# A transformer encoder on one core: the sums of the second and third down steps each wait for another pair's split

## The chip, the cores and the metric

The kernel runs on 1 core of one Trainium2 chip. The metric is the device time of one execution in microseconds (us); lower is better. A program on a core drives several engines that run side by side, each with an in-order queue of its own: TensorE (PE; its weight loads are listed as PEld), VectorE (DVE), ScalarE (ACT), GpSimd (POOL) and SyncE (SP), the last of which only issues DMA transfers here.

## The reference

Two encoder layers over 256 tokens of width 2048. Each layer has a token mixer (neighbourhood attention in the first, grouped-query attention in the second) beside cross-attention to 256 memory tokens, one output projection, and then a dense MLP with a squared ReLU. The change is in the MLP:

```python
        n = rms_norm(h, mlp_norm[i])
        h = h + jnp.square(jax.nn.relu(n @ w_up[i])) @ w_down[i]
```

`w_up` is 2048 x 8192 and `w_down` 8192 x 2048, in float32.

## The kernel before, in words

**Split products.** Every float32 operand is split into a rounded high part (ACT copies it to the reduced type) and the residual (DVE subtracts the high part from the original); the helper `split` does both, so all its rows carry lines L507 (ACT) and L508 (DVE). A product is then three matmuls: high x high, high x low, low x high. Names end accordingly: `uh`/`ul` for the up weights, `bh`/`bl` and `th`/`tl` for the down weights, `a_s` for the activations.

**The up products.** `w_up` comes in 64 chunks of 128 features (`up_grains`). A chunk is loaded to `raw_U`, split in two halves, and multiplied in 48 matmuls of 128x256 (L411) into `ps_u`. Then ACT applies ReLU and square (L1113, L1114) into a tile `c`. Two consecutive chunks make a **pair**; when its second chunk is done, `squared` forms sums and differences of its four 128x128 blocks on DVE (L1122 to L1124) and splits them into `a_s`. The residual of that split (on DVE) is the instruction that the program notes in `box["made"]`.

**The down products.** Most of `w_down` is done by a Strassen scheme: 60 down **steps** (`down_grains`, numbered n from 0), each with one pair and one 1024-column half of the output. A step loads a tile `b` of four 128x512 blocks and makes a tile `t` of four sums from it: one block by an ACT copy (L1165) and an accumulating DMA issued by POOL (L1166), the other three by DVE in a chain, L1172, L1173, L1174, each reading the one before. Three blocks of `b` are split into `bh`, `bl` and used in the step's first half (9 matmuls of 128x512 on PE); the four sums are split into `th`, `tl` and used in its second half (12 matmuls; L1195, L1198 and L1199 are the three matmuls of a product). The products go to seven accumulators `p1` to `p7` in PSUM. When the output half changes, they are evacuated by ACT (copies to `z`, L1250) and by DVE (L1241). The buffers of `bh`, `bl`, `th` and `tl` are single: the next step's split waits until PE has read the last one. `t` has two buffers, `b` three.

**The order of work.** The MLP begins with four up chunks; from then on step n is interleaved with one up chunk: first half of the step, two halves of up chunk n + 4, second half. PE's order is pinned (`keep_in_program_order`). On the other engines a scheduler of the framework orders the instructions when the kernel is built, from its own estimate of the times; `tc.issue_after(x)` forbids it to put the instructions inside it ahead of instruction x on the same engine. It is used in `pre`, where the first of the three sums (L1172) is built, for n = 1 and n = 2, the second and the third step: L1173 and L1174 follow it through their data. Step n takes the pair j of `STEPS[n]`; the run lengths in `RUNS` begin with two steps on one output half and then alternate by four, so the first steps use the pairs 0, 1, 0, 1, 2, 3.

Of the kernel before, what the change touches and what calls it, by code (L numbers as in the profile page):

```python
# [159 lines left out]
def encoder_kernel(ctx: ExitStack, tc: tile.TileContext, t: dict, out: bass.AP):  # L160
# [206 lines left out]
    def later(n, fn, *args):  # L367
        pending.append((state["tick"] + n, fn, args))
# [136 lines left out]
    def split(dst_hi, dst_lo, src):  # L505

        first = nc.scalar.activation(dst_hi, src, AF.Copy)  # L507
        return first, nc.vector.tensor_tensor(dst_lo, src, dst_hi.bitcast(F32), op=ALU.subtract)  # L508
# [422 lines left out]
    def past(fn, ins=None):  # L931

        a, v = ins or box["ready"]
        with tc.issue_after(a.ins), tc.issue_after(v.ins):
            fn()
# [112 lines left out]
    def up_grains(layer, m):  # L1048
# [50 lines left out]
        def after():  # L1099
            squared(layer, m, own["ps"])  # L1100
# [5 lines left out]
    def squared(layer, m, ps):  # L1106

        e = m % 2
        if e == 0:
            box["c"] = at.mlp.tile([P, 8, P], F32, tag="c", bufs=2, name="c")  # L1110
        c = box["c"]
        two = c[:, 2 * e : 2 * e + 2, :].rearrange("p a b -> p (a b)")
        box["relu"] = nc.scalar.activation(two, ps, AF.Relu)  # L1113
        nc.scalar.activation(two, two, AF.Square)  # L1114
        if e == 0:
            return
        pair = m // 2
        if pair >= max(STEPPED):
            a = at.mlp.tile([P, 2, 4, P], F32R, tag="a", bufs=6, name="a_p")
            split(a[:, 0], a[:, 1], c[:, :4])  # L1120
        else:
            nc.vector.tensor_tensor(c[:, 4, :], c[:, 0, :], c[:, 2, :], op=ALU.subtract)  # L1122
            nc.vector.tensor_tensor(c[:, 5:7, :], c[:, 0:8:4, :], c[:, None, 1, :].to_broadcast([P, 2, P]), op=ALU.add)
            nc.vector.tensor_tensor(c[:, 7, :], c[:, 3, :], c[:, 6, :], op=ALU.subtract)  # L1124
            a = at.mlp.tile([P, 2, 7, P], F32R, tag="a", bufs=6, name="a_s")
            box["made"] = split(a[:, 0], a[:, 1], c[:, 1:])[1]
            if pair >= min(STEPPED):

                n = pair - min(STEPPED)
                if n == 0:  # L1130
                    box["a_0"] = at.mlp.tile([P, max(STEPPED) - min(STEPPED), 2, P], F32R, tag="a", bufs=6, name="a_0")
                split(box["a_0"][:, n, 0], box["a_0"][:, n, 1], c[:, 0])
        box["a", pair] = a
        if m == UPS - 1 and layer == 1:
            later(2, load_gf)
# [11 lines left out]
    def down_grains(layer, n, begins, ends, sooner):  # L1147

        q, j = STEPS[n]
        own = {}  # L1150

        def load():
            own["b"] = at.side.tile([P, 4, 512], F32, tag="b", bufs=3, name="b")
            nc.sync.dma_start(own["b"].rearrange("p a b -> p (a b)"),
                              t[f"w_pair{layer}"][j * 2 + q])

        def behind(fn, far=4):

            return (lambda: past(fn, box["splits"][-far])) if n < 2 else fn

        def lift():

            b, s = own["b"], at.side.tile([P, 4, 512], F32, tag="T", bufs=2, name="t")
            own["t"] = s
            nc.scalar.activation(s[:, 3, :], b[:, 3, :], AF.Copy)  # L1165
            nc.gpsimd.dma_start(s[:, 3, :], b[:, 1, :], accum_op=ALU.add)  # L1166

        def pre():

            b, s = own["b"], own["t"]  # L1170
            with tc.issue_after(box["made"].ins) if n in (1, 2) else nullcontext():
                nc.vector.tensor_tensor(s[:, 0, :], b[:, 3, :], b[:, 0, :], op=ALU.add)  # L1172
            nc.vector.tensor_tensor(s[:, 1, :], s[:, 0, :], b[:, 1, :], op=ALU.add)  # L1173
            nc.vector.tensor_tensor(s[:, 2, :], s[:, 1, :], b[:, 2, :], op=ALU.add)  # L1174

        def prep_first():
            own["first"] = tuple(at.mlp.tile([P, 3 * 512], F32R, tag=x, name=x) for x in ("bh", "bl"))
            split(*own["first"], own["b"].rearrange("p a b -> p (a b)")[:, : 3 * 512])

        def prep_second():  # L1180
            own["second"] = tuple(at.mlp.tile([P, CH], F32R, tag=x, name=x) for x in ("th", "tl"))
            with tc.issue_after(box["relu"].ins) if n == 0 else nullcontext():
                split(*own["second"], own["t"].rearrange("p a b -> p (a b)"))

        def run(which, products):
            if n == 0 and which == "first":
                open_strassen(layer)
            hi, lo = own.pop(which)
            a = box["a", j]
            for name, ai, bi in products:  # L1190
                if n == 0:
                    sum_of(name)
                entered = begins and not (name in SHARED and q in box["z_set"])
                ps, s = box["ps"][name], slice(bi * 512, (bi + 1) * 512)
                ins = nc.tensor.matmul(ps, a[:, 0, ai, :], hi[:, s], start=entered, stop=False,  # L1195
                                       skip_group_check=True)
                pin(ins)
                nc.tensor.matmul(ps, a[:, 0, ai, :], lo[:, s], start=False, stop=False, skip_group_check=True)  # L1198
                nc.tensor.matmul(ps, a[:, 1, ai, :], hi[:, s], start=False, stop=ends, skip_group_check=True)  # L1199

        def after(products):
            if ends:
                for name, _, _ in products:
                    taken(q, name)
                    if n + 1 < len(STEPS):
                        seeded(STEPS[n + 1][0], name)

        def after_second():
            after(SECOND)
            if ends:  # L1210
                box["z_set"].add(q)
            if ends and j == STEPPED[q] - 1:
                folded(q, 0.5 if n == len(STEPS) - 1 else 1)

        return [Grain(lambda: run("first", FIRST), lambda: after(FIRST), load, behind(pre), behind(prep_first, 4 if n else 1),
                      (8 if n < 2 else 12, 8 if sooner else 5, 4), behind(lift)),
                Grain(lambda: run("second", SECOND), after_second, None, None, behind(prep_second), SOONER)]

    def open_strassen(layer):

        closed(*[x for x in reversed(list(pools)) if x in ("ps_acc", "ps_att")])
        at.sums = opened("ps_sums", space=bass.MemoryType.PSUM)
        first = ["p3", "p5", "p1", "p2"]
        second = ["up"] + [x[0] for x in SECOND[:3]]
        box["ps"], box["unused"] = {}, set()
        for x in first + second if layer else second + first:
            box["ps"][x] = at.sums.tile([P, 512], F32, tag=x, name="ps_u" if x == "up" else x)
            box["unused"].add(x)

    def sum_of(name):  # L1230
        if name in box["unused"]:
            box["unused"].remove(name)
        else:
            box["ps"][name] = at.sums.tile([P, 512], F32, tag=name, name="ps_u" if name == "up" else name)
        return box["ps"][name]
# [7 lines left out]
    def taken(q, name):  # L1243

        ps, inv = box["ps"][name], box["inv"]
        if name in DIRECT:
            i, b = DIRECT[name]
            add_scaled(columns_of(i, q, b), ps, inv[:, i : i + 1])
            return
        nc.scalar.activation(box["z"][q][:, SHARED.index(name), :], ps, AF.Copy)  # L1250

    def seeded(q, name):

        ps = sum_of(name)
        if name in SHARED and q in box["z_set"]:
            nc.scalar.activation(ps, box["z"][q][:, SHARED.index(name), :], AF.Copy)
# [524 lines left out]
```

## Time and profile before

| what | value |
|---|---|
| median of 3 runs | 2002.78 us (2001.56 to 2003.46) |
| the profiled execution, time | 2002.76 us |
| its span | 2001.0 us |
| mean granted clock of TensorE | 0.997 |
| PE busy | 1984.8 us, 99% of the span |
| DVE busy | 1726.2 us, 86% |
| ACT busy | 1443.1 us, 72% |
| POOL busy | 149.9 us, 7% |

The span runs from the first to the last instruction. The page of the profile gives shares over the whole span; a wait is shown in the timeline in brackets behind the instruction that waited, with the instruction that released it. In a timeline row the first number is the start in us from the beginning of the span, the second the duration, and "x2" stands for two instructions merged into one row. Starts of successive DVE instructions can be closer than the duration of one, since they overlap a little. The first layer's down steps begin at 442.2 us, the second layer's at 1350.7.

### The profile page before, as it was taken

The page shows a single profiled execution, that of the slowest core. Times are in us where ns is not written, and L with a number is a line of the kernel's source. Part 1 is how long each engine was busy: PE and PEld are TensorE (multiplying, and loading weights), DVE is VectorE, ACT ScalarE, POOL GpSimd, SP SyncE. Part 2 cuts the span into 40 slices and gives each one's busy share as a digit, 9 for nine tenths or more (in the row PEclk, how much of TensorE's full clock was granted, in tenths as well). Part 3 has the DMA queues.
Part 4 walks back from the last instruction along what each step waited for, and adds up shares of the span by engine and source line. Part 5 has one row for each costly group of instructions (what it writes and reads, how often), then busy time and mean ns, then how long its engine had stood idle before and what let it go on. Part 6 is the DMA issues. An engine that isn't in the chain of part 4 may idle for free.

```text
span 2001.0 us, 33096 instructions
## 1 busy us (share of the span) xinstructions
PE 1984.8 (99%) x12832; PEld 1801.8 (90%) x12832; DVE 1726.2 (86%) x2096; ACT 1443.1 (72%) x2105; POOL 149.9 (7%) x205
## 2 busy tenths in 40 slices
PE   9999999999999999999999999999999999999998
PEld 9999999898999999999998888898999999999997
DVE  6777767579999999999999869778999999999997
ACT  6655555577887788877887666667788777877786
POOL 0000000000000000000001011000000000000001
PEclk9999999999999999999999999999999999999999
DMA  7855555667777777777778765667777777777775
GB/s 288 320 193 204 206 192 185 261 211 217 223 228 237 234 235 235 221 241 226 229 227 229 263 216 174 225 202 229 226 226 230 237 231 231 237 226 243 228 225 152
DMA packets 110685, 452.46 MB, mean 226 GB/s; under 512 B 18880, under 2 KB 40640, under 8 KB 63168
## 3 DMA queue, kind: packets, MB, share of 16 engines
q1 hardware_dynamic: 90144, 413.38, 60.3%
q0 software_dynamic: 20096, 36.45, 10.4%
q8 instruction: 100, 1.64, 0.3%
q14 instruction: 57, 0.47, 0.1%
q10 hardware_dynamic: 288, 0.52, 0.1%
HBM read 397.78 MB, written 4.19 MB: 201 GB/s over the span
## 4 chain that ended last, share of the span: by engine, by line
PE 98%; DVE 1%; ACT 1%; issue 0%; POOL 0%; DVEq 0%; POOLq 0%
PE ps_u L411 35%; PE p L1198 10%; PE p L1199 10%; PE p L1195 10%; PE ps_s L411 9%; PE ps_m L391 8%; PE ps_m L392 8%; PE ps_m L388 7%; PE sc_ps L604 0%; PE sc_ps L605 0%; PE sc_ps L603 0%; PE av L696 0%; PE av L697 0%; PE av L698 0%; PE idle L240 0%
## 5 line engine op out<-in xcount | busy, mean ns | idle before, releaser
L411 PE MATMUL ps_u<-hT,uh 128*128 128x256 f32 x3874 | 674.5, 276 | 0.0
L411 PEld LDWEIGHTS ps_u<-hT,uh 128*128 128x128 f32 x3874 | 588.5, 188 | 5.8
L411 PE MATMUL ps_u<-hT,ul 128*128 128x256 f32 x1994 | 550.7, 276 | 0.0
L507 ACT ACTIVATE uh<-raw_U 128x1024 fp32r<-128x1024 f32 x262 | 277.5, 1060 | 154.3 <-PE ps_u L411 149.8
L411 PEld LDWEIGHTS ps_u<-hT,ul 128*128 128x128 f32 x1994 | 374.3, 188 | 0.0
L507 ACT ACTIVATE hi<-raw 128x1024 fp32r<-128x1024 f32 (+1 forms) x215 | 222.0, 1037 | 183.0 <-PE ps_m L392 94.2
L508 DVE TENSOR_TENSOR lo<-raw,hi 128x1024 fp32r<-128x1024 f32 (+1 forms) x215 | 255.0, 1190 | 108.4 <-ACT hi L507 107.7
L508 DVE TENSOR_TENSOR ul<-raw_U,uh 128x1024 fp32r<-128x1024 f32 x262 | 319.6, 1220 | 15.7 <-ACT uh L507 15.7
L508 DVE TENSOR_TENSOR tl<-t,th 128x2048 fp32r<-128x2048 f32 x120 | 274.7, 2290 | 57.5 <-ACT th L507 57.3
L507 ACT ACTIVATE th<-t 128x2048 fp32r<-128x2048 f32 x120 | 230.8, 1924 | 90.4 <-PE p L1199 90.4
L508 DVE TENSOR_TENSOR bl<-b,bh 128x1536 fp32r<-128x1536 f32 x120 | 210.3, 1752 | 0.3 <-ACT bh L507 0.3
L1198 PE MATMUL p<-tl,a_s 128*128 128x512 f32 x480 | 188.9, 394 | 5.7 <-DVE tl L508 5.7
L1166 POOL DMA_DIRECT2D t<-b x120 | 104.2, 869 | 1169.4 <-ACT t L1165 1113.2
L1195 PE MATMUL p<-th,a_s 128*128 128x512 f32 x480 | 188.8, 393 | 0.2
L1199 PE MATMUL p<-th,a_s 128*128 128x512 f32 x480 | 188.0, 392 | 0.0
L507 ACT ACTIVATE bh<-b 128x1536 fp32r<-128x1536 f32 x120 | 178.6, 1488 | 3.7
L411 PE MATMUL ps_s<-nT,hi 128*128 128x256 f32 x896 | 154.6, 277 | 0.0
L1199 PE MATMUL p<-bh,a_s 128*128 128x512 f32 x360 | 140.9, 391 | 0.0
L1198 PE MATMUL p<-bl,a_s 128*128 128x512 f32 x360 | 140.1, 389 | 0.0
L1195 PE MATMUL p<-bh,a_s 128*128 128x512 f32 x360 | 140.1, 389 | 0.0
L411 PEld LDWEIGHTS ps_s<-nT,hi 128*128 128x128 f32 x896 | 135.3, 188 | 0.2
L411 PE MATMUL ps_s<-nT,lo 128*128 128x256 f32 x448 | 124.2, 277 | 0.0
(292 smaller groups left out, 3639.9 us busy)
## 6 DMA issues: line engine op xcount, KB each, us to landing
raw_U<-in_w_up SPq DMA_DIRECT2D x128, 1024.0 KB, 6.3
b<-in_w_pair SPq DMA_DIRECT2D x120, 1024.0 KB, 5.8
raw<-in_w_o SPq DMA_DIRECT2D x32, 1024.0 KB, 5.0
t<-b POOLq DMA_DIRECT2D x120, 256.0 KB, 6.5
raw<-in_w_b SPq DMA_DIRECT2D x21, 1024.0 KB, 5.7
raw<-in_w_av SPq DMA_DIRECT2D x12, 1024.0 KB, 5.0
raw<-in_w_aq SPq DMA_DIRECT2D x12, 1024.0 KB, 5.0
raw<-in_w_ak SPq DMA_DIRECT2D x12, 1024.0 KB, 4.9
```

What stands on the lines that cost most here:

```text
L388: first = nc.tensor.matmul(ps, ah, hi[:, s], start=st, stop=False)
L391: nc.tensor.matmul(ps, ah, lo[:, s], start=False, stop=False)
L392: final = nc.tensor.matmul(ps, al, hi[:, s], start=False, stop=sp)
L411: ins = nc.tensor.matmul(ps, x, acts[:, k, part], start=k == n == 0, stop=k == KT - 1 and n == 2)
L507: first = nc.scalar.activation(dst_hi, src, AF.Copy)
L508: return first, nc.vector.tensor_tensor(dst_lo, src, dst_hi.bitcast(F32), op=ALU.subtract)
L1166: nc.gpsimd.dma_start(s[:, 3, :], b[:, 1, :], accum_op=ALU.add)
L1195: ins = nc.tensor.matmul(ps, a[:, 0, ai, :], hi[:, s], start=entered, stop=False, skip_group_check=True)
L1198: nc.tensor.matmul(ps, a[:, 0, ai, :], lo[:, s], start=False, stop=False, skip_group_check=True)
L1199: nc.tensor.matmul(ps, a[:, 1, ai, :], hi[:, s], start=False, stop=ends, skip_group_check=True)
```

## The change

`box["made"]` held the last activation split that had been built, whichever pair it belonged to. Now each pair's split is noted under its own number, and the sums of step n wait for the split of pair n - 1: those of the second step (n = 1) for the first pair's, those of the third (n = 2) for the second pair's. When the sums of both steps are built, the second pair's split is the last one, so both waited for that before.

```diff
             a = at.mlp.tile([P, 2, 7, P], F32R, tag="a", bufs=6, name="a_s")
-            box["made"] = split(a[:, 0], a[:, 1], c[:, 1:])[1]
+            box["made", pair] = split(a[:, 0], a[:, 1], c[:, 1:])[1]
...
             b, s = own["b"], own["t"]
-            with tc.issue_after(box["made"].ins) if n in (1, 2) else nullcontext():
+            with tc.issue_after(box["made", n - 1].ins) if n in (1, 2) else nullcontext():
                 nc.vector.tensor_tensor(s[:, 0, :], b[:, 3, :], b[:, 0, :], op=ALU.add)
```

The scheduler's order follows. PE's and POOL's orders are the same; SP has one load moved ahead of another in each layer; DVE and ACT differ in a stretch of some 30 instructions per layer, and what is shown here for the first layer holds for the second as well.

DVE behind the split of the first pair (`a_s_4780`). `t_4817` is the tile of sums of the second step, `t_4957` that of the third, `b_4815` and `b_4922` are what they are made from; `ul_4854` and `ul_4887` are the two halves of the fifth up chunk, and `tl_4928` is the residual of the first step:

```order
 L508 TENSOR_TENSOR a_s_4780<-c_4713,a_s_4780 128x896
+L1172 TENSOR_TENSOR t_4817<-b_4815 128x512
+L1173 TENSOR_TENSOR t_4817<-t_4817,b_4815 128x512
 L508 TENSOR_TENSOR ul_4854<-raw_U_4716,uh_4853 128x1024
+L1174 TENSOR_TENSOR t_4817<-t_4817,b_4815 128x512
 L508 TENSOR_TENSOR ul_4887<-raw_U_4716,uh_4886 128x1024
 L508 TENSOR_TENSOR tl_4928<-t_4683,th_4927 128x2048
```

The three sums of the second step now stand here, two ahead of the first residual of the up chunk and one ahead of the second.

DVE behind the split of the second pair (`a_s_4919`). `tl_5054` is the residual of the second step's sums, `bl_5076` that of the third step's `b`, `ul_5107` a residual of the seventh up chunk:

```order
 L508 TENSOR_TENSOR a_s_4919<-c_4848,a_s_4919 128x896
-L1172 TENSOR_TENSOR t_4817<-b_4815 128x512
 L1172 TENSOR_TENSOR t_4957<-b_4922 128x512
 L974 TENSOR_TENSOR inv_5027<-full_5025,near_4417 128x2
 L508 TENSOR_TENSOR ul_5033<-raw_U_4851,uh_5032 128x1024
-L1173 TENSOR_TENSOR t_4817<-t_4817,b_4815 128x512
 L1173 TENSOR_TENSOR t_4957<-t_4957,b_4922 128x512
 L976 TENSOR_SCALAR ninv_5030<-inv_5027 128x2
 L1241 SCALAR_TENSOR_TENSOR first_83<-p3_4940,inv_5027,first_83 128x512
+L1174 TENSOR_TENSOR t_4957<-t_4957,b_4922 128x512
 L1241 SCALAR_TENSOR_TENSOR first_83<-p2_4943,inv_5027,first_83 128x512
-L1174 TENSOR_TENSOR t_4817<-t_4817,b_4815 128x512
-L1174 TENSOR_TENSOR t_4957<-t_4957,b_4922 128x512
+L508 TENSOR_TENSOR tl_5054<-t_4817,th_5053 128x2048
 L508 TENSOR_TENSOR bl_5076<-b_4922,bh_5075 128x1536
 L508 TENSOR_TENSOR ul_5107<-raw_U_4988,uh_5106 128x1024
-L508 TENSOR_TENSOR tl_5054<-t_4817,th_5053 128x2048
```

The second step's sums are gone from here, the third step's stay, and `tl_5054` stands ahead of `bl_5076` and `ul_5107` instead of behind them.

ACT in the same place, as it stands now. `th_5053` is the high part that `tl_5054` needs, `bh_5075` that of `bl_5076`:

```order
L1114 ACTIVATE c_5020<-c_5020 128x256
L507 ACTIVATE th_5053<-t_4817 128x2048
L1250 ACTIVATE z1_4653<-p1_4942 128x512
L507 ACTIVATE bh_5075<-b_4922 128x1536
L1077 ACTIVATE u_0_5110<-raw_U_4988 128x128
L507 ACTIVATE uh_5106<-raw_U_4988 128x1024
```

Before, `th_5053` stood behind `uh_5106`, four places later.

## Prediction

> **What bounds the kernel now.** I read the first and fourth parts of the page, then the waits of TensorE, then its timeline where it waits.
>
> ```profile
> span 2001.0 us, 33096 instructions
> PE 1984.8 (99%) x12832; PEld 1801.8 (90%) x12832; DVE 1726.2 (86%) x2096; ACT 1443.1 (72%) x2105; POOL 149.9 (7%) x205
> PE 98%; DVE 1%; ACT 1%; issue 0%; POOL 0%; DVEq 0%; POOLq 0%
> PE p L1198 <- DVE tl L508: 5.7, 2, 2.8
> ```
>
> TensorE (PE) is the bound nearly everywhere. It has one kind of wait for another engine's work inside the program: the residual `tl`, twice, 2.8 us each. These are the second halves of the second down step of each layer, so what the change can give or take lies there. The PE timeline around both places (start, duration, operation):
>
> ```profile
> 454.76 0.28 PE L411 MATMUL ps_u<-hT,u 128*128 128x256 f32 x1
> 460.09 0.28 PE L411 MATMUL ps_u<-hT,ul 128*128 128x256 f32 x1
> 460.48 0.50 PE L1195 MATMUL p<-th,a_s 128*128 128x512 f32 x1
> 463.82 0.50 PE L1198 MATMUL p<-tl,a_s 128*128 128x512 f32 x1 [2.84 <-DVE tl L508]
> 465.14 0.63 PE L1199 MATMUL p<-th,a_s 128*128 128x512 f32 x1
> 465.57 0.63 PE L1195 MATMUL p<-th,a_s 128*128 128x512 f32 x1
> 470.07 0.28 PE L411 MATMUL ps_u<-hT,u 128*128 128x256 f32 x1
> 1363.28 0.28 PE L411 MATMUL ps_u<-hT,u 128*128 128x256 f32 x1
> 1378.63 0.28 PE L411 MATMUL ps_u<-hT,u 128*128 128x256 f32 x1
> ```
>
> The undisturbed rhythm is in the chain of waits, one line per up chunk:
>
> ```profile
> 470.23 5.45 PE ps_u L411 x48
> 480.46 5.45 PE ps_u L411 x48
> ```
>
> One step (48 up matmuls, then 12 of a second half and 9 of the next first half) takes 10.23 us: 5.45 for the up chunk, 4.78 for the 21 down matmuls (0.2275 each). At the stall it takes 470.07 - 454.76 = 15.31 in the first layer and 1378.63 - 1363.28 = 15.35 in the second. The loss is 5.08 + 5.12 = **10.2 us**, more than the 5.7 us of recorded waiting. In the first layer it divides so. The first matmul on `th` starts at 460.48 where the rhythm (0.11 behind the last up matmul) would have it at 460.20: 0.28. The next, on `tl`, starts 3.34 later instead of 0.23: 3.11. From there the next up chunk is 6.25 away, where 20 matmuls need 4.55: 1.70. That last term is no wait: behind the stall matmuls start 0.43 apart (465.14, 465.57) where the rhythm has 0.23, and the granted clock says why (stretch, PE and PEld busy with counts, DVE, ACT, POOL, clock, DMA share, GB/s):
>
> ```profile
> 465.00:470.00 5.00, 5.00 (x17) 3.97 (x17) 4.11 (x8) 3.50 (x5) 0.60 (x1) 0.71 0.78 209
> 480.00:520.00 40.00, 40.00 (x273) 36.81 (x273) 36.76 (x38) 31.67 (x43) 3.47 (x4) 1.00 0.74 230
> ```
>
> **What makes tl late.** VectorE (DVE) and ScalarE (ACT) in the first layer:
>
> ```profile
> 441.39 1.22 DVE L508 TENSOR_TENSOR ul<-raw_U,uh 128x1024 fp32r<-128x1024 f32 x1
> 443.39 1.23 DVE L508 TENSOR_TENSOR ul<-raw_U,uh 128x1024 fp32r<-128x1024 f32 x1 [0.79 <-ACT uh L507]
> 445.47 2.29 DVE L508 TENSOR_TENSOR tl<-t,th 128x2048 fp32r<-128x2048 f32 x1 [0.85 <-ACT th L507]
> 451.49 1.07 DVE L508 TENSOR_TENSOR a_s<-c,a_s 128x896 fp32r<-128x896 f32 x1
> 452.48 1.29 DVE L1172 TENSOR_TENSOR t<-b 128x512 f32<-128x512 f32 x2
> 454.89 1.29 DVE L1173 TENSOR_TENSOR t<-t,b 128x512 f32<-128x512 f32 x2
> 456.16 1.40 DVE L1241 SCALAR_TENSOR_TENSOR first<-p,inv,first 128x512 f32<-128x512 f32 x2
> 457.48 1.28 DVE L1174 TENSOR_TENSOR t<-t,b 128x512 f32<-128x512 f32 x2
> 458.68 1.75 DVE L508 TENSOR_TENSOR bl<-b,bh 128x1536 fp32r<-128x1536 f32 x1
> 460.35 1.22 DVE L508 TENSOR_TENSOR ul<-raw_U,uh 128x1024 fp32r<-128x1024 f32 x1
> 461.49 2.28 DVE L508 TENSOR_TENSOR tl<-t,th 128x2048 fp32r<-128x2048 f32 x1
> 437.30 0.63 ACT L1165 ACTIVATE t<-b 128x512 f32<-128x512 f32 x1 [0.70 <-DMA b<-in_w_pair]
> 452.53 0.42 ACT L1114 ACTIVATE c<-c 128x256 f32<-128x256 f32 x1
> 458.53 1.90 ACT L507 ACTIVATE th<-t 128x2048 fp32r<-128x2048 f32 x1
> 444.43 0.19 PEld L411 LDWEIGHTS ps_u<-hT,ul 128*128 128x128 f32 x1
> ```
>
> Behind the second pair's `a_s` at 451.49 no row shows idle time up to 463.77. The sums of both steps (x2 on each line) stand behind the second pair's split; `th` on ACT needs the second step's sums, which end at 457.48 + 0.68 = 458.16; and `tl` comes behind all of it. From 442.6 to 445.47, on the other hand, DVE idles 0.79 and 0.85.
>
> **The change, part by part.** No operation is added or removed; per layer three sums (128x512, 0.60 us from start to start, 1.29 for two) move ahead, and the instructions behind them close up.
>
> (1) *The sums in their new place.* They stand behind the first `a_s`, two of them ahead of the first `ul` of that chunk. The second reads what the first wrote with nothing between, and such a pair starts no sooner than the first ends: 0.68 + 0.04, the 0.04 from the next rows (a chain on `c`).
>
> ```profile
> 438.28 0.29 DVE L1122 TENSOR_TENSOR c<-c 128x128 f32<-128x128 f32 x1 [0.45 <-ACT c L1114]
> 438.60 0.42 DVE L1123 TENSOR_TENSOR c<-c 128x256 f32<-128x256 f32 x1
> ```
>
> So sums at 441.39 and 442.11, `ul` 442.71 to 443.93, third sum 443.85, second `ul` 444.45, `tl` of the first step at 445.59 instead of 445.47. Of 0.72 + 0.60 + 0.60 = 1.92 us, 1.80 falls into the two idle times or what opens beside them; 0.12 is left over. Cover: PE loads the first `ul` at 444.43, so 0.50 us is left there, the thinnest margin of the change. The sums read `b`, which had landed at 437.30, when ACT's copy of it began. Cost on PE: nothing; with the cover gone, the overrun itself plus up to 1.7 of slow clock.
>
> (2) *What is taken off the way to tl.* Between the second `a_s` and the second step's `tl` fall away: three sums (1.80), `bl` (458.68 to 460.35, 1.67) and `ul` (460.35 to 461.49, 1.14), the latter two because the scheduler now puts `tl` ahead of them. That is 4.61: `tl` starts at 461.49 - 4.61 + 0.12 = 457.0 and ends at 459.3. PE wants it at 460.20 + 0.23 = 460.43. Margin 1.1 us.
>
> (3) *th on ACT* moves ahead of the copy of `z` and of `bh`. Its buffer is free when PE has read the first step's:
>
> ```profile
> 452.48 0.39 PE L1199 MATMUL p<-th,a_s 128*128 128x512 f32 x1
> 457.56 1.06 ACT L507 ACTIVATE uh<-raw_U 128x1024 fp32r<-128x1024 f32 x1 [0.92 <-PE ps_u L411]
> ```
>
> So 452.87, and the copy before it on ACT ends at 452.95: `th` from 453.0 to 454.9, 2.1 us before `tl` needs it. Behind it `z` and `bh` slip some 0.6 us, which the 0.92 us of idle before `uh` takes. Gain at the first matmul: the 0.28.
>
> (4) *What is late next.* The `bl` and `ul` that were passed: `bl` 459.2 to 461.0, wanted by PE at 460.20 + 12 x 0.2275 = 462.9; `ul` 460.9 to 462.1, wanted at 465.0. Then `tl` of the third step. Between come a second `ul` (1.14), three sums (1.8), one L1241 (0.7) and two small operations on `c` (0.29 and 0.42 in the rows above): it starts near 466.3 and ends at 468.6; PE wants it at 460.20 + 10.23 + 0.23 = 470.66. Margin 2.0. The fourth `tl` stands in the old order.
>
> (5) *Queues.* On SP the load of the fifth `b` moves ahead of one `raw_U` load. Its buffer is free after the second step's sums and `bl`, and with the sums early the `bl` decides: 447.88 + 1.75 = 449.63 instead of the 458.19 of the next rows. The accumulating transfer of the third step's `t` then shares the DMA engines with it; such transfers took the times of the last row:
>
> ```profile
> 447.88 1.75 DVE L508 TENSOR_TENSOR bl<-b,bh 128x1536 fp32r<-128x1536 f32 x1
> 458.19 2.60 SPq L1154 DMA_DIRECT2D b<-in_w_pair  x2
> 448.72 0.86 POOL L1166 DMA_DIRECT2D t<-b  x1 [9.60 <-ACT t L1165]
> DMA to landing us min/median/max: 3.9/7.2/9.5
> ```
>
> At the longest, 9.5, it lands at 458.2, and the third step's `th` starts no sooner than 463. Nothing. POOL's order is unchanged.
>
> *Sum:* -(0.28 + 3.11 + 1.70) in the first layer, -5.12 in the second, +0 elsewhere: -10.2 us, for the profiled run 2002.76 - 10.2 and its span 1990.8. That run stands 0.02 below the median 2002.78. The unknown price is a residue of the stall. Below: none, nothing beyond the 10.2 can be had, since PE has no other wait. Above: a wait of half a microsecond in each layer that brings the slow clock along, 2 x (0.5 + 1.7) = 4.4 us. I take none, nearest to the row of the undisturbed step, and keep the 4.4 for the range.
>
> [...]
>
> **Rivals.**
> *A, the stall moves on or stays in part.* DVE does not idle from 451 to 466 in the new order as well, and every margin in (2) and (4) is estimated to a few tenths. If `tl` of the second or third step comes over 1 to 2 us later than worked out, PE stalls 0.5 and runs slow: 2002.8 - 10.2 + 4.4 = 1997.0. For it: DVE is busy 36.76 of 40 us even in the undisturbed stretch. Against: both margins are above 1 us and no input is missing.
> *B, the change does nothing for PE.* `tl` would be late by its `th` or a transfer, and not by its place; 2002.8. Against: `th` is done at 454.9 by (3).
> *C, slower.* The sums block DVE ahead of the first `ul`. The place is 441.39; it decides once `b` lands after 441.9 (0.50 us of margin). It is net slower once the new loss passes the old one, 5.1 - 1.7 = 3.4 later, at 445.3. With `b` landing at 447.4, PE would lose 5.5 + 1.7 per layer at the up chunk in place of 5.1 later: 2002.8 + 2 x 2.1 = 2007.0. Against: `b` had landed 4.1 us before.
>
> **The numbers.** Forecast 0.80, A 0.10, B 0.06, C 0.04. About 0.2% (4 us) is what a measurement of this kernel can tell from no change. The forecast and A lie beyond it on the fast side: 0.90 faster; B the same, and of C a part that stays within 4 us: 0.07 same; 0.03 slower. Predicted 1992.6 us. The low end is 1991.0, the full gain with the spread of the three runs (1.2 below their median) and a little more; the high end 1997.3 takes in A.
>
> **What would show it.** Right: no PE wait on `tl` at L1198; the distance from the second up chunk of the steps to the third 10.2 instead of 15.3 in both layers; clock 1.00 throughout those stretches; `th` of the second step near 453, its `tl` near 457; the first `ul` behind the first `a_s` ending near 443.9 with no PE wait there. Wrong: a PE wait on `ul` near 444.4 (C), on `tl` of the third step near 470 (A), or an unchanged stall (B).

## The result, and the profile after

| | median | lowest to highest | executions |
|---|---|---|---|
| before | 2003.02 us | 2001.56 to 2003.46 | 4 |
| after | 1992.22 us | 1992.13 to 1993.13 | 4 |

The ratio is 0.9948, with a 95% interval of 0.9931 to 0.9966: the change makes the kernel 10.8 us faster. The forecast was 1992.6. On another chip, with 5 executions after and 11 before, it was 1992.81 against 2002.96, 0.9946 (0.9933 to 0.9960).

The span and the first part of the page of the changed kernel, and the view of what TensorE waited for (line waited for: us in total, times, longest):

```profile
span 1990.4 us, 33096 instructions
PE 1979.7 (99%) x12832; PEld 1798.3 (90%) x12832; DVE 1726.2 (87%) x2096; ACT 1442.7 (72%) x2105; POOL 149.9 (8%) x205
PE idle L240 <- POOL mhalf L234: 1.0, 1, 1.0
PE ps_s L411 <- ACT hi L507: 0.5, 1, 0.5
```

The waits for `tl` are gone, and no other wait stands in their place in the MLP: the two that are left belong to other parts of the program and lie in the first 8 us of the execution. DVE's work is unchanged (1726.2 us in both).

TensorE's timeline at the place of the first stall, and at the same place in the second layer:

```profile
454.41 0.28 PE L411 MATMUL ps_u<-hT,u 128*128 128x256 f32 x1
459.86 0.40 PE L1195 MATMUL p<-th,a_s 128*128 128x512 f32 x1
460.09 0.39 PE L1198 MATMUL p<-tl,a_s 128*128 128x512 f32 x1
464.64 0.28 PE L411 MATMUL ps_u<-hT,u 128*128 128x256 f32 x1
1357.86 0.28 PE L411 MATMUL ps_u<-hT,u 128*128 128x256 f32 x1
1368.09 0.28 PE L411 MATMUL ps_u<-hT,u 128*128 128x256 f32 x1
```

From one up chunk to the next it is now 10.23 in both layers (464.64 - 454.41 and 1368.09 - 1357.86), the undisturbed rhythm, where it was 15.31 and 15.35. The matmul on `tl` follows the one on `th` after 0.23 instead of 3.34. The granted clock in the two stretches of 5 us that the stall had marked (the first number behind the five engines; 0.95 and 0.71 before):

```profile
460.00:465.00 5.00, 5.00 (x26) 4.17 (x25) 5.00 (x8) 4.77 (x7) 0.64 (x1) 1.00 0.81 220
465.00:470.00 5.00, 5.00 (x47) 5.00 (x46) 5.00 (x6) 4.19 (x6) 0.68 (x1) 1.00 0.62 256
```

So the account of the profiled executions closes: 2002.76 - 1992.20 = 10.56. Of it 5.08 + 5.12 = 10.20 lie in the two steps. Another 0.35 is there before the steps begin (the up chunk that started at 454.76 starts at 454.41, and up matmuls that started at 431.33, ahead of everything that moved, start at 430.98), in a part of the program that the change does not touch.

VectorE and ScalarE around the changed places:

```profile
440.82 0.69 DVE L1172 TENSOR_TENSOR t<-b 128x512 f32<-128x512 f32 x1
441.54 0.69 DVE L1173 TENSOR_TENSOR t<-t,b 128x512 f32<-128x512 f32 x1
442.15 1.22 DVE L508 TENSOR_TENSOR ul<-raw_U,uh 128x1024 fp32r<-128x1024 f32 x1
444.08 0.19 PEld L411 LDWEIGHTS ps_u<-hT,ul 128*128 128x128 f32 x1
445.12 2.29 DVE L508 TENSOR_TENSOR tl<-t,th 128x2048 fp32r<-128x2048 f32 x1
452.56 1.92 ACT L507 ACTIVATE th<-t 128x2048 fp32r<-128x2048 f32 x1
456.54 2.28 DVE L508 TENSOR_TENSOR tl<-t,th 128x2048 fp32r<-128x2048 f32 x1
458.74 1.75 DVE L508 TENSOR_TENSOR bl<-b,bh 128x1536 fp32r<-128x1536 f32 x1
465.68 2.29 DVE L508 TENSOR_TENSOR tl<-t,th 128x2048 fp32r<-128x2048 f32 x1
449.31 0.33 SPq L1154 DMA_DIRECT2D b<-in_w_pair  x1
```

The second step's first two sums stand at 440.82 and 441.54. The `ul` behind them ends at 443.37, and PE loads it at 444.08: 0.71 us to spare. `th` stands at 452.56, and `tl` runs from 456.54 to 458.82, 1.27 ahead of the matmul at 460.09. The third step's `tl` ends at 467.97; PE takes it at 470.32, 2.35 later.

### The profile page after: what moved, and what is told of

Same layout as the page of the kernel before. It is cut to its first block, busy times and chain, and to the rows that moved or that the text cites. A ratio compares the mean times of both kernels' runs of the same rounds, so it can differ in the third digit from the quotient of the medians.

```text
span 1990.4 us, 33096 instructions
## 1 busy us (share of the span) xinstructions
PE 1979.7 (99%) x12832; PEld 1798.3 (90%) x12832; DVE 1726.2 (87%) x2096; ACT 1442.7 (72%) x2105; POOL 149.9 (8%) x205
## 4 chain that ended last, share of the span: by engine, by line
PE 99%; DVE 0%; DMA 0%; issue 0%; SPq 0%; DVEq 0%; ACT 0%; POOLq 0%; POOL 0%
PE ps_u L411 35%; PE ps_s L411 10%; PE p L1195 10%; PE p L1199 10%; PE p L1198 10%; PE ps_m L391 8%; PE ps_m L392 8%; PE ps_m L388 8%; DMA raw<-in_w_first 0%; PE sc_ps L603 0%; PE sc_ps L605 0%; PE sc_ps L604 0%; PE av L696 0%; PE av L697 0%; PE av L698 0%; PE av L690 0%
```

## The experiments

In all of them the kernel computes the same output; in those that delay `tl`, part or all of that residual is computed twice.

**The change again.** The kernel after as it is, on one chip with the next experiment's second kernel and, of the delays below, the one of 2048 columns without the `ul`.

> The changed kernel itself again, beside the two that follow. Theory: 1992.2 and a spread below 1 us, because no wait of TensorE is left that could bring the slow clock. Rival (chips differ, the 1992.2 belongs to another chip): 1993 or more.

Measured: 1992.81 (1992.01 to 1993.33). The spread is 1.3 us, a little more than said. It is the base for what ran on that chip. Its profiled execution (1992.81) has no recorded wait of a matmul in the MLP, but one of a weight load in the first layer:

```profile
443.27 1.22 DVE L508 TENSOR_TENSOR ul<-raw_U,uh 128x1024 fp32r<-128x1024 f32 x1
444.55 0.19 PEld L411 LDWEIGHTS ps_u<-hT,ul 128*128 128x128 f32 x1 [0.29 <-DVE ul L508]
```

`b` came later there (ACT's copy, which waited for it, begins at 437.86 instead of 436.74), the first `ul` behind the sums ended at 444.49, and PE's load of it waited 0.29. The margin of 0.71 was gone. The next up chunk came 10.95 behind that one instead of 10.45; the other part of this loss lies at the second pair's `a_s`, whose residual ended at 453.23, when PE could have used it at 453.08.

**One layer at a time.** The first kernel makes the change in the first layer only, the second in the second layer only; the other layer's sums wait as before.

```diff
-            with tc.issue_after(box["made", n - 1].ins) if n in (1, 2) else nullcontext():
+            with tc.issue_after(box["made", n - 1 if layer == 0 else 1].ins) if n in (1, 2) else nullcontext():
```

> The change in the first layer only; in the second layer the sums of both steps wait for the second pair's split as before. Forecast's theory: the two stalls are separate and worth 5.1 us each (5.08 and 5.12 in the trace before), so 1992.2 + 5.1 = 1997.3; TensorE waits once for tl, 2.8 us, in the second layer and not at all in the first. Rival (the gain is one thing for the whole program, or the first layer's stall comes back later): anything else than half, 1992.2 or 2002.8; a wait for tl in the first layer.

> The change in the second layer only, the counterpart of the one in the first layer only (1998.35 median, 1994.8 to 1999.4). Theory 1 (each layer's stall costs 5.1, as in the profiled run): 1992.2 + 5.1 = 1997.3. Theory 2 (the slow clock behind a stall comes in some executions and not in others, more often or longer in the second layer, so that its median is 6.1 and the first layer's 4.4): 1996.7, and a spread of several us between executions in both.

Measured: the first layer only 1998.35 (1994.79 to 1999.38; 2002.78 before, on that chip), the second only 1997.60 (1995.05 to 1999.34; 2002.96 before). The change in the first layer alone gains 4.43, in the second alone 5.36, together 9.79, where both at once gain 10.15 on the second's chip. The gain is two separate stalls, each worth about half. Theory 1 of the second expectation (1997.3) is 0.3 off the measured 1997.60 and 1.05 off the 1998.35; theory 2 has the direction right (4.43 against 5.36) but overstates it (1996.7). Both medians lie within a spread of over 4 us, so the split between the layers is not known better than to about 1 us.

The spread itself is the finding. Both kernels have one recorded wait of TensorE in the MLP, of the same length. TensorE there, with the second layer's stall left (first three rows) and with the first layer's left (the next four, and its windows' row from 465 to 470):

```profile
1366.69 0.50 PE L1198 MATMUL p<-tl,a_s 128*128 128x512 f32 x1 [2.84 <-DVE tl L508]
1367.02 0.40 PE L1199 MATMUL p<-th,a_s 128*128 128x512 f32 x1
1372.98 0.28 PE L411 MATMUL ps_u<-hT,u 128*128 128x256 f32 x1
454.63 0.28 PE L411 MATMUL ps_u<-hT,u 128*128 128x256 f32 x1
463.69 0.79 PE L1198 MATMUL p<-tl,a_s 128*128 128x512 f32 x1 [2.83 <-DVE tl L508]
464.28 0.63 PE L1199 MATMUL p<-th,a_s 128*128 128x512 f32 x1
471.03 0.28 PE L411 MATMUL ps_u<-hT,u 128*128 128x256 f32 x1
465.00:470.00 5.00, 5.00 (x14) 3.83 (x14) 4.07 (x7) 3.29 (x5) 0.46 (x1) 0.56 0.83 227
```

In the first case the matmul behind the stall still takes 0.40, the full-speed duration, and the next up chunk comes 6.29 after the stalled matmul. In the second the stalled matmul itself already takes 0.79, the clock from 465 to 470 is 0.56, and it is 7.34 to the next up chunk. That step took 471.03 - 454.63 = 16.40, a loss of 6.17, for a wait that cost 5.08 in the profile before.

**The order on VectorE alone.** The sums stay late as before; only `bl` of the third step is put behind `tl` of the second. The arguments of one call are left out in the diff.

```diff
-            with tc.issue_after(box["made", n - 1].ins) if n in (1, 2) else nullcontext():
+            with tc.issue_after(box["made", 1].ins) if n in (1, 2) else nullcontext():
...
-            split(*own["first"], own["b"].rearrange("p a b -> p (a b)")[:, : 3 * 512])
+            with tc.issue_after(box["second", 1][1].ins) if n == 2 else nullcontext(): split(*own["first"], ...)
...
-                split(*own["second"], own["t"].rearrange("p a b -> p (a b)"))
+                box["second", n] = split(*own["second"], own["t"].rearrange("p a b -> p (a b)"))
```

> The sums stay late as before (both steps behind the second pair's split); only the split bl of the third step's first half is put behind tl of the second step on VectorE. Forecast's theory (tl is late because th is, and th because the sums are): th still ends at 460.4, tl then from 460.5 to 462.75, TensorE waits about 2.1 us instead of 3.1 in each layer; the 0.28 at th stays. 2000.8 if the slow clock behind the stall stays, 1997.6 if the shorter wait does not bring it. Rival (the order on VectorE alone is what matters, the sums' place nothing): 1992.2 to 1994.

Measured: 1998.51 (1997.43 to 2000.98), 4.3 below before and 6.3 above the change (1992.22, on another chip). ScalarE, VectorE and TensorE in the first layer, then TensorE in the second, and the clock in both:

```profile
457.67 1.90 ACT L507 ACTIVATE th<-t 128x2048 fp32r<-128x2048 f32 x1
459.60 2.29 DVE L508 TENSOR_TENSOR tl<-t,th 128x2048 fp32r<-128x2048 f32 x1 [0.33 <-ACT th L507]
453.90 0.28 PE L411 MATMUL ps_u<-hT,u 128*128 128x256 f32 x1
461.95 0.50 PE L1198 MATMUL p<-tl,a_s 128*128 128x512 f32 x1 [1.82 <-DVE tl L508]
466.66 0.28 PE L411 MATMUL ps_u<-hT,u 128*128 128x256 f32 x1
1359.88 0.28 PE L411 MATMUL ps_u<-hT,u 128*128 128x256 f32 x1
1367.93 0.50 PE L1198 MATMUL p<-tl,a_s 128*128 128x512 f32 x1 [1.83 <-DVE tl L508]
1374.20 0.28 PE L411 MATMUL ps_u<-hT,u 128*128 128x256 f32 x1
465.00:470.00 5.00, 5.00 (x39) 4.68 (x38) 5.00 (x7) 4.83 (x6) 0.00 (x0) 1.00 1.00 341
1365.00:1370.00 5.00, 3.06 (x12) 2.10 (x11) 4.44 (x4) 3.41 (x6) 0.86 (x1) 0.83 0.47 193
```

Counted as the expectation counts it, from start to start (TensorE's first matmul on `th` stood at 459.62, so 2.33 less 0.23), the wait is 2.10, as expected. The median lies between the two times given, and in the profiled execution the clock came down behind one stall of the two. Two things follow. `tl` still waits for `th` (0.33 us, released by ACT), and `th` for the late sums: order on VectorE alone gets less than half of the gain, and the rest needs the sums ahead, as step (2) and step (3) of the prediction say. And with waits of 1.82 and 1.83 us in one execution the clock stayed at 1.00 behind the first and fell to 0.83 behind the second. The steps took 12.76 and 14.32, losses of 2.53 and 4.09: the slow clock was 1.56 of the second, and nothing of the first.

**Sums earlier still.** In the first kernel the sums of both steps wait for the first pair's split, in the second no sums wait for any split.

```diff
-            with tc.issue_after(box["made", n - 1].ins) if n in (1, 2) else nullcontext():
+            with tc.issue_after(box["made", 0].ins) if n in (1, 2) else nullcontext():
```

```diff
-            with tc.issue_after(box["made", n - 1].ins) if n in (1, 2) else nullcontext():
+            with tc.issue_after(box["made", n - 1].ins) if n in () else nullcontext():
```

> The sums of both steps wait for the first pair's split only. Then the third step's sums stand ahead of the second pair's activation split on VectorE. Forecast's theory (the sums of a step must come early enough for their own residual, and no earlier than the work that TensorE wants first): the second pair's a_s residual, which ends at 452.2 with 0.6 us to spare in the profile after, comes some 3 us later, TensorE's first half on it waits about 2.4 us in each layer, and the time is 1992.2 + 2 x 2.4 = 1997.0, up to 2000.4 where the slow clock comes with the wait (1.7 per layer). Rival (only the lateness of the second step's sums mattered, VectorE has room for the third step's sums anywhere): 1992.2.

> No sums wait for any split. Then the second step's sums go ahead of the first pair's split as well, where they wait in the first layer for their load (landed at 436.7). Forecast's theory: the first pair's a_s comes about 1 us late for TensorE in the first layer, the second pair's as in the kernel where both wait for the first pair; 1997 to 2000.4. Rival C of the prediction (early sums block VectorE ahead of work that TensorE wants sooner) says the same with a loss that may exceed the gain: up to 2007. Rival (the waits at the sums are needless, VectorE hides them all): 1992.2.

Measured: 1999.98 (1997.60 to 2001.90) and 2000.95 (1998.80 to 2003.89). The first kernel, VectorE, ScalarE and TensorE in the first layer:

```profile
451.72 0.68 DVE L1173 TENSOR_TENSOR t<-t,b 128x512 f32<-128x512 f32 x1
452.64 0.95 ACT L507 ACTIVATE a_s<-c 128x896 fp32r<-128x896 f32 x1 [0.75 <-DVE c L1124]
454.40 1.07 DVE L508 TENSOR_TENSOR a_s<-c,a_s 128x896 fp32r<-128x896 f32 x1
443.91 0.28 PE L411 MATMUL ps_u<-hT,u 128*128 128x256 f32 x1
453.64 0.50 PE L1195 MATMUL p<-bh,a_s 128*128 128x512 f32 x1 [1.17 <-ACT a_s L507]
455.52 0.50 PE L1199 MATMUL p<-bh,a_s 128*128 128x512 f32 x1 [1.15 <-DVE a_s L508]
457.25 0.28 PE L411 MATMUL ps_u<-hT,u 128*128 128x256 f32 x1
```

The third step's sums now stand among the differences of the second pair and ahead of its `a_s`, whose high part ends at 453.59 and whose residual at 455.47 (by the expectation some 3 us after 452.2). PE waits for both in its first half. The step takes 457.25 - 443.91 = 13.34 where the change has 443.96 to 454.41, 10.45: 2.9 lost, without a slow clock. In the profiled execution (1997.60) the clock fell nowhere near these waits (1.00 from 455 to 475), in others it may have: 2001.9 at most. The lowest execution, which is the profiled one, lies 0.6 above the expectation's lower figure, 1997.0, and the median is in the bounds that it gave for a slow clock.

Without any wait for a split, the second step's sums also stand ahead of the first pair's `a_s`, two of them ahead of the differences it is made from:

```profile
437.53 0.69 DVE L1172 TENSOR_TENSOR t<-b 128x512 f32<-128x512 f32 x1 [1.27 <-DMA b<-in_w_pair]
442.98 1.09 DVE L508 TENSOR_TENSOR a_s<-c,a_s 128x896 fp32r<-128x896 f32 x1 [1.02 <-ACT a_s L507]
443.00 0.50 PE L1195 MATMUL p<-bh,a_s 128*128 128x512 f32 x1 [0.32 <-ACT a_s L507]
455.09 0.50 PE L1195 MATMUL p<-bh,a_s 128*128 128x512 f32 x1 [0.66 <-ACT a_s L507]
456.98 0.50 PE L1199 MATMUL p<-bh,a_s 128*128 128x512 f32 x1 [1.16 <-DVE a_s L508]
457.78 0.63 PE L1199 MATMUL p<-bh,a_s 128*128 128x512 f32 x1
```

This is the mechanism of rival C, made real: sums that wait for their load (1.27 us) hold up VectorE's queue, and PE waits for what stands behind. At the second pair it then waits as in the kernel above, and here the matmuls behind the two waits take 0.63 instead of 0.40: the slow clock, granted 0.78 from 455 to 460 and 0.88 from 460 to 465. It did not come to 2007, the price at which rival C was put for a load landing ten microseconds later; 2000.95 is a little above the upper end of what the forecast's theory had, 2000.4, and against the 2002.78 before on that chip no difference is shown (ratio 0.9992, 0.9982 to 1.0001). The rival that VectorE hides them all is out. Each step's sums have a range of places that cost nothing: behind the pair that PE needs next, ahead of their own residual.

**How late may tl be?** The same change, with an extra residual of 1024, 1536 or 2048 columns directly ahead of `tl` of the second step, so that `tl` comes later; `bl` of the third step is kept behind `tl` by the guard of the experiment on the order. The added residual and `tl` stand on L1183 here. With 2048 columns the scheduler also puts one `ul` between the two; a further kernel, whose expectation is the third below, forbids that. The diff is for 1024 columns, with one long line written out and without that guard:

```diff
-                split(*own["second"], own["t"].rearrange("p a b -> p (a b)"))
+                hi, lo = own["second"]; x = own["t"].rearrange("p a b -> p (a b)")
+                nc.scalar.activation(hi, x, AF.Copy)
+                if n == 1: nc.vector.tensor_tensor(lo[:, :1024], x[:, :1024], hi[:, :1024].bitcast(F32), op=ALU.subtract)
+                box["second", n] = nc.vector.tensor_tensor(lo, x, hi.bitcast(F32), op=ALU.subtract)
```

> The changed kernel with one more residual of 1024 columns (about 1.2 us of VectorE, no other effect) directly ahead of tl of the second step, and bl of the third step kept behind tl. The margin of tl in the profile after is 1.27 us. Theory: 1992.2, no wait of TensorE above 0.1 us. Rival (the margin is less than it looks, or later margins are used up): 1992.5 or more.

> The same with 1536 columns (about 1.7 us): tl comes 0.4 to 0.5 us late for TensorE in each layer. Theory of the trace's terms (a wait brings the slow clock along): up to 1992.2 + 2 x (0.45 + 1.7) = 1996.5. Rival (a short wait costs itself and no slow clock): 1993.1.

> The changed kernel with one more residual of 2048 columns (2.28 us) directly ahead of tl of the second step, and both bl of the third step and the ul that had slipped ahead kept behind tl: tl comes 2.28 + 0.04 - 1.27 = 1.05 us late in each layer, between the 0.55 that brought no slow clock (1993.8) and the 2.1 that brought it in some executions (1996.1 to 2001.3). If 1.05 brings none: 1992.2 + 2.1 = 1994.3 in every execution. If it brings it in some: a spread from 1994.3 up to 1997.7.

> The same with 2048 columns (2.28 us), behind which one ul (1.14) also slips ahead of tl: tl comes about 3.4 - 1.27 = 2.1 us late in each layer. If such a wait brings the slow clock: 1992.2 + 2 x (2.1 + 1.7) = 1999.8; if not, 1996.4.

TensorE's wait in the first layer, in the order 1536, 2048, and 2048 with the `ul` (with 1024 none of 0.1 or more is recorded); then the clock of the last in the first layer and in the second:

```profile
461.13 0.50 PE L1198 MATMUL p<-tl,a_s 128*128 128x512 f32 x1 [0.65 <-DVE tl L1183]
460.97 0.50 PE L1198 MATMUL p<-tl,a_s 128*128 128x512 f32 x1 [1.20 <-DVE tl L1183]
462.78 0.50 PE L1198 MATMUL p<-tl,a_s 128*128 128x512 f32 x1 [1.95 <-DVE tl L1183]
465.00:470.00 5.00, 5.00 (x23) 4.17 (x22) 3.49 (x8) 3.12 (x4) 0.00 (x0) 0.81 1.03 303
1370.00:1375.00 5.00, 4.33 (x12) 3.46 (x13) 5.00 (x7) 1.83 (x3) 0.86 (x1) 0.66 0.45 72
```

| extra residual | recorded wait, layers 1 and 2 | loss of the step | clock behind it | median | lowest to highest |
|---|---|---|---|---|---|
| none | 0, 0 | 0, 0 | 1.00 | 1992.22 and 1992.81 | 1992.0 to 1993.3 |
| 1024 | 0, 0 | 0.40, 0.16 | 1.00 | 1992.74 | 1992.0 to 1993.0 |
| 1536 | 0.65, 0.41 | 0.96, 0.73 | 1.00 | 1993.78 | 1993.6 to 1994.2 |
| 2048 | 1.20, 0.94 | 1.48, 1.27 | 1.00 | 1994.70 | 1994.1 to 1995.4 |
| 2048 and `ul` | 1.95, 2.36 | 3.88, 4.28 | 0.81, 0.66 | 1999.56 | 1996.1 to 2001.3 |

The loss of a step is the distance of its two up chunks in the profiled execution, less 10.23. The margin of 1.27 read off the profile after is confirmed to a few tenths: with 1024 columns `tl` ends some 0.2 behind the rhythm in the first layer, more than expected. The median, 1992.74, meets the rival's number (1992.5 or more) but cannot be told from the 1992.81 of the change on another chip. From 1024 to 2048 columns (without the `ul`) the added residual takes 1.07 us more on VectorE (2.32 against 1.25), and the step loses 1.08 more in the first layer and 1.11 in the second. These waits without a slow clock cost themselves and about 0.3 more (0.31, 0.32, 0.28 and 0.33), since the wait is counted from the end of the matmul before it (0.50 after its start), where in the rhythm the next one starts 0.23 behind it. Waits up to 1.20 brought no slow clock in the profiled executions, and the spread of the others, 1.3 us or below, shows no sign of one. Waits of about 2 brought it in both layers of the profiled execution (2001.30), some 1.6 each; the lowest execution (1996.14) agrees with none.

## Why the prediction was right

The forecast came true at each of its steps; starts in the profile after are 0.35 earlier than in the profile before, which the differences below contain.

- **The sum.** Predicted -10.2; the two steps measured -10.20, the profiled executions -10.56, the medians -10.8 and -10.15.
- **(1) The sums in their new place.** First `ul` predicted until 443.93, 0.50 ahead of its load; measured 443.37 and 0.71. First step's `tl` predicted at 445.59, measured 445.12. No wait of PE came of it in this profile. In that of the repetition this margin, which the prediction called the thinnest, was used up, and the step took 0.5 us longer.
- **(2) tl.** Predicted 457.0 to 459.3 with 1.1 to spare; measured 456.54 to 458.82 and 1.27. The delay experiment shows that this margin is real.
- **(3) th.** Predicted at 453.0, measured 452.56. The experiment on the order alone shows that this step carries a good part of the gain: with `th` late, `tl` first in the queue still brought a wait of 1.8.
- **(4) What is late next.** `bl` predicted until 461.0, measured 460.49; third step's `tl` until 468.6 with 2.0 to spare, measured 467.97 and 2.35. Rival A did not come.
- **(5) Queues.** The fifth `b` predicted at 449.63, measured 449.31, without a wait elsewhere.

**What was wrong in it** is the price of the residue, "a wait of half a microsecond in each layer that brings the slow clock along, 2 x (0.5 + 1.7) = 4.4 us". The runs show 0.96 and 0.73 for waits of 0.65 and 0.41, clock 1.00, 1.6 us in the median over the changed kernel's 1992.22 (another chip; 1.0 over the 1992.74 of the smallest delay on the same one). Of the two times expected for that run (1536 columns), 1993.1 without a slow clock was nearer to the measured 1993.78 than the up to 1996.5 with one. The high end of the range and rival A's 1997.0 rested on the 4.4, so they were too high for a half microsecond. A slow clock of about 1.6 per layer did come, but with waits of about two (median 1999.56).

The 1.70 of slow clock in the first layer was a term of the sum, and it came out right because that very execution was its base. It is no constant: 1.70 in the profile before, 2.78 behind the same wait with the change in the second layer only (6.17 less 0.28 and 3.11). The executions before that stood beside the first set of experiments spread from 1999.92 to 2004.27 (31 of them), those of the change over 1.3 us.

A margin that the prediction did not name is that of the second pair's `a_s`. It was there before, but it is the one that limits how early the sums can stand, as the kernel with both steps' sums behind the first pair's split shows.

## What to carry to other kernels

When two engines' work is tied together by an order constraint, give each piece its own: the sums of a step should stand as late as their own consumer allows and no earlier than what TensorE needs before it; one guard for two steps made the earlier one late, and with no guard the work that TensorE needs first came late. Read the cost of a stall from the distance of undisturbed work on both sides of it (10.2 us here), not from the recorded wait (5.7). Here a late input that left TensorE waiting for 0.94 and 1.20 us cost 1.27 and 1.48; one that left it waiting for 1.95 and 2.36 cost 3.88 and 4.28, and differently from one execution to the next (1996.14 to 2001.30). Two short waits 1.9 us apart brought the clock down in one place (0.66 and 1.16 us) and not in another (1.17 and 1.15); a single one of 1.20 did not.

## What the runs showed of the hardware

The granted clock does not answer to the length of a wait alone. Behind single recorded waits of 0.41 to 1.20 us it stayed at 1.00 (four of them in profiles). Of pairs of waits 1.9 us apart, 1.17 and 1.15 left it at 1.00, and 0.66 and 1.16 brought it down (0.78 from 455 to 460, 0.88 from 460 to 465). Behind 1.82 it stayed, behind 1.83 of the same execution it fell (0.83). Behind 1.95 to 2.84 it fell in every profile, for a price of 1.6 to 2.8 us, twice before the stalled matmul had ended (0.79, and 0.76 in the second layer before, instead of 0.50) and once only after the next ones had run at full speed (0.40).

In the profile before, read in stretches of 0.05 us around the two stalls, the clock is 0.50 from 464.47 to 467.88 and from 1372.42 to 1375.83, and 1.00 ahead of both and behind both. TensorE is busy throughout the two slow stretches. At half the clock 3.41 us of busy TensorE lose 1.7, the price there (1.70 in the first layer). What decides whether a wait brings the clock down, and for how long, was not shown.
